# A one-core log-softmax over 50000 columns: the first tile's load cut into four column pieces, and one late store issued inside the next tile's exponentials

## The chip, the cores and the metric

The kernel runs on one core of one Trainium2 chip. The metric is the device time of one execution in microseconds (us). The seven runs of the kernel before took 7582.85, 7583.15, 7583.72, 7608.13, 7610.33, 7612.80 and 7635.38 us; their median is 7608.13 us. Besides them one execution was taken by the profiler, and every duration below comes from that one.

## The reference

The input is `x` with 16 x 512 x 50000 values in float32, so 8192 rows of 50000 columns, 1638.4 MB in and as much out.

```python
max_x = np.max(x, axis=-1, keepdims=True)
shifted = x - max_x
log_sum_exp = np.log(np.sum(np.exp(shifted), axis=-1, keepdims=True))
return (shifted - log_sum_exp).astype(np.float32)
```

## The kernel before

A tile is 32 rows. Each row is cut into four segments of 12500 columns, and each segment lies on a partition of its own, so a tile is 128 partitions x 12500 values, 6250 KB (50 KB a partition). There are 256 tiles, numbered 0 to 255 here, and four buffers (`NBUF`), each of a whole tile; a tile is loaded into its buffer, changed in place and stored from it. For the vector work a tile has four column pieces (`NS`) of 3125 columns, which `cols(c)` picks.

The order of the work is written by hand, engine by engine, with semaphores:

- SyncE (SP) issues the loads. Tiles 0 to 3 are loaded at once, each whole with one `dma_start` that raises `landed[j]` by 16. From then on, in a loop of 63 rounds over the four buffers, it waits for `stored[j]`, takes 16 off it and loads the next tile into buffer j. So load t+4 is issued when store t has landed.
- VectorE (DVE), in `whole(j)`, waits for `landed[j]` (through `take`, line 45), reduces each of the four pieces to a negated maximum (line 195), joins the four (line 200), shares the maximum among the four partitions of a row by transposes (`share`, lines 163 to 178), later multiplies the partial sums by their scales (line 206), and subtracts maximum and log-sum from the whole buffer with one instruction (line 183). In the last tile alone that subtraction is cut into four pieces.
- ScalarE (ACT), in its own `whole(j)`, takes the exponential of each piece with its own maximum and adds it up (line 234, one exponential behind each reduction), makes the scales (line 242) and the logarithm (line 225). After that it issues the store of the tile (line 229, `store`), which waits until DVE has subtracted. The store of the last tile goes out in four pieces.
- TensorE adds the four segments of a row by a matrix of ones (line 271).

Loads and stores are issued on two queues: the page's q1 carries the loads and q10 the stores. Each has its own transfers in order, and the 16 DMA engines work on both.

DVE and ACT run 63 rounds of four tiles in loops; the last four tiles (252 to 255) are written out behind the loops. Tile 252 is the fourth-last.

A count of events on a semaphore is kept by `Count`: `next` makes an instruction wait for the next event, so two instructions that wait on `subtracted` take its events in the order in which they are written.

Of the kernel before, what the change touches and what calls it, by code (L numbers as in the profile page):

```python
# [19 lines left out]
NBUF = 4  # L20

NS = 4


class Count:
# [17 lines left out]
def take(engine, sem, n=16):  # L43

    engine.wait_ge(sem, n).then_inc(sem, -n)  # L45


def cols(c):
    return slice(c * C, (c + 1) * C)
# [3 lines left out]
def kernel(  # L53
# [9 lines left out]
    W = V // G  # L63
    assert N % R == 0 and W == NS * C
    ntiles = N // R


    rounds = (ntiles - NBUF) // NBUF
    assert ntiles % NBUF == 0 and rounds >= 2

    xt = xf.rearrange("(t r) (g w) -> t (r g) w", r=R, g=G)
    ot = of.rearrange("(t r) (g w) -> t (r g) w", r=R, g=G)

    def run(a, first, n):

        part = a[first : first + NBUF * n].rearrange("(q i) p w -> q i p w", i=NBUF)
        return lambda q, i: part[bass.ds(q, 1), i].rearrange("o p w -> (o p) w")
# [13 lines left out]
    bufs = [data.tile([P, W], FP32, name=f"buf{j}") for j in range(NBUF)]  # L91
# [4 lines left out]
    def each(n, width, name):  # L96
        return [stats.tile([P, width], FP32, name=f"{name}{j}") for j in range(n)]

    negms, parts, scales, scaleds = (
        each(NBUF, NS, n) for n in ("negm", "part", "scale", "scaled")  # L100
    )
# [9 lines left out]
    def sem(name):  # L111
        return ctx.enter_context(nc.semaphore(name))

    landed = [sem(f"landed{j}") for j in range(NBUF)]
    stored = [sem(f"stored{j}") for j in range(NBUF)]
    ready = sem("ones_ready")
    on_dve = Count(sem("on_dve"))
    on_act = Count(sem("on_act"))
# [10 lines left out]
    @block.gpsimd  # L129
    def _(gpsimd):  # L130
        view = ones.rearrange("p (r g) -> p r g", g=G)
        gpsimd.memset(ones, 1.0).then_inc(ready)  # L132
        gpsimd.affine_select(  # L133
            out=view, in_=view, pattern=[[-G, R], [0, G]], base=0,
            channel_multiplier=1, compare_op=ALU.is_ge, fill=0.0,
        ).wait_op(ready, 1, "sem-ge").then_inc(ready)
        gpsimd.affine_select(  # L137
            out=view, in_=view, pattern=[[G, R], [0, G]], base=G - 1,
            channel_multiplier=-1, compare_op=ALU.is_ge, fill=0.0,
        ).wait_op(ready, 2, "sem-ge").then_inc(ready)  # L140

    @block.sync
    def _(sync):
        def load(j, src):
            sync.dma_start(out=bufs[j], in_=src).then_inc(landed[j], 16)

        for t in range(NBUF):
            load(t, xt[t])
        src = run(xt, NBUF, rounds)
        with sync.Fori(0, rounds) as q:  # L150
            for j in range(NBUF):
                take(sync, stored[j])
                load(j, src(q, j))
        for j in range(NBUF - 1):
            take(sync, stored[j])
        take(sync, stored[NBUF - 1], 16 * NS)

    @block.vector
    def _(vector):
        def share(k):  # L160

            on_dve.next(
                vector.transpose(out=allneg, in_=negp.to_broadcast([P, SQ]))  # L163
            ).then_inc(on_dve.sem)
            on_dve.next(
                vector.tensor_reduce(  # L166
                    out=rowneg, in_=allneg.rearrange("p (r g) -> p r g", g=G),
                    op=ALU.min, axis=AX,
                )
            ).then_inc(on_dve.sem)  # L170
            on_dve.next(
                vector.tensor_copy(  # L172
                    out=spread.rearrange("p (r g) -> p r g", g=G),
                    in_=rowneg[:, :, None].to_broadcast([P, SQ // G, G]),
                )
            ).then_inc(on_dve.sem)
            on_dve.next(
                vector.transpose(out=negmaxs[k], in_=spread)  # L178
            ).then_inc(agreed.sem)

        def subtract(k, *bufs):
            for n, buf in enumerate(bufs):
                ins = vector.tensor_scalar(  # L183
                    out=buf, in0=buf, scalar1=negmaxs[k][:, 0:1], scalar2=logs[k],
                    op0=ALU.add, op1=ALU.subtract,
                )
                if n == 0:
                    logged.next(ins)
                ins.then_inc(subtracted.sem)

        def whole(j, by_pieces=False):
            take(vector, landed[j])

            for c in range(NS):
                vector.tensor_reduce(  # L195
                    out=negms[j][:, c : c + 1], in_=bufs[j][:, cols(c)],
                    op=ALU.max, axis=AX, negate=True,
                ).then_inc(shifted.sem if c < NS - 1 else on_dve.sem)
            on_dve.next(vector.nop()).then_inc(shifted.sem)  # L199
            vector.tensor_reduce(  # L200
                out=negp, in_=negms[j], op=ALU.min, axis=AX
            ).then_inc(on_dve.sem)
            share(j)

            rescaled.next(
                vector.tensor_mul(out=scaleds[j], in0=scales[j], in1=parts[j])  # L206
            ).then_inc(summed.sem)
            subtract(j, *([bufs[j][:, cols(c)] for c in range(NS)] if by_pieces else [bufs[j]]))

        def settle():  # L210
            for count in (on_dve, rescaled, logged):
                count.settle(vector)

        with vector.Fori(0, rounds):
            for j in range(NBUF):
                whole(j)
            settle()
        for j in range(NBUF):
            whole(j, by_pieces=j == NBUF - 1)

    @block.scalar
    def _(scalar):
        def log(k):
            added.next(
                scalar.activation(out=logs[k], in_=rowsums[k], func=ACT.Ln)  # L225
            ).then_inc(logged.sem)

        def store(j, dst, buf):
            subtracted.next(scalar.dma_start(out=dst, in_=buf)).then_inc(stored[j], 16)

        def whole(j):
            for c in range(NS):
                shifted.next(
                    scalar.activation(  # L234
                        out=dump, in_=bufs[j][:, cols(c)], func=ACT.Exp,
                        bias=negms[j][:, c : c + 1], scale=1.0,
                        accum_out=parts[j][:, c : c + 1],
                    )
                ).then_inc(on_act.sem)
                on_act.next(scalar.nop())  # L240
            agreed.next(
                scalar.activation(  # L242
                    out=scales[j], in_=negms[j], func=ACT.Exp,
                    bias=negmaxs[j][:, 0:1], scale=-1.0,
                )
            ).then_inc(rescaled.sem)
            log(j)

        def settle():
            for count in (on_act, shifted, agreed, added, subtracted):  # L250
                count.settle(scalar)

        nc.scalar.preload_act_table_set("natural_log_exp_and_others")  # L253
        dst = run(ot, 0, rounds)
        with scalar.Fori(0, rounds) as q:
            for j in range(NBUF):
                whole(j)
                store(j, dst(q, j), bufs[j])
            settle()
        for j in range(NBUF - 1):  # L260
            whole(j)
            store(j, ot[ntiles - NBUF + j], bufs[j])
        whole(NBUF - 1)
        for c in range(NS):
            store(NBUF - 1, ot[ntiles - 1][:, cols(c)], bufs[NBUF - 1][:, cols(c)])
# [50 lines left out]
```

## Time and profile before

| what | value |
|---|---|
| median of the seven runs | 7608.13 us (7582.85 to 7635.38) |
| the profiled execution's own time | 7599.88 us |
| its span, first to last instruction | 7598.2 us |
| VectorE busy | 5441.1 us (72%) |
| ScalarE busy | 3184.7 us (42%) |
| TensorE matmul busy | 477.7 us (6%) |
| reductions, line 195 | 1024 of 3.40 us |
| exponentials, line 234 | 1024 of 2.87 us |
| whole-tile subtraction, line 183 | 6.79 us each |
| bytes moved | 1638.4 MB read, 1638.4 MB written |
| load, issue to landing, median | 44.1 us |
| whole-tile store, issue to landing, median | 48.0 us |

The page gives for each engine its busy time as a share of the span. Below that it cuts the span into 40 slices of 190 us and gives for each the mean busy share of the 16 DMA engines in tenths and the rate at which they moved bytes. The time from issue to landing of a transfer includes the time that it waits in its queue behind the transfer issued before it, and it ends when the last of the 16 engines has moved its part.

### The profile page before, as it was taken

To read this page: it belongs to the slowest core of one execution; us is meant where nothing else is said; L and a number is where in the kernel's file an instruction comes from. 1 tells how busy PE (TensorE), PEld (TensorE's weight loads), DVE (VectorE), ACT (ScalarE), POOL (GpSimd) and SP (SyncE) were. 2 spreads that over 40 slices of the span, in tenths; PEclk is the share of its full clock that TensorE was granted. 3 is DMA by queue.
4 is the path that set the end of the run, shared out by engine and by line. 5 is a ranking of instruction groups with operands and counts; after the bars stand their busy time and mean duration, and the time that the engine had idled before them with its cause. 6 is when DMAs were issued, how large, how long until landed. Compare 5 with 4: busy or idle time off the path is not lost. (4 is left out here: it accounts for less than half of the span.)

```text
span 7598.2 us, 14069 instructions
## 1 busy us (share of the span) xinstructions
PE 477.7 (6%) x2048; PEld 455.8 (6%) x2048; DVE 5441.1 (72%) x2819; ACT 3184.7 (42%) x2561; POOL 1.4 (0%) x7
## 2 busy tenths in 40 slices
PE   0000000000000000000000000000000000000000
PEld 0000000000000000000000000000000000000000
DVE  7777777777777777777777777777777777777776
ACT  4444344443434434344443444434344443444433
POOL 0000000000000000000000000000000000000000
DMA  9999999999999999999999999999999999999998
GB/s 415 433 434 434 434 434 434 434 434 434 432 434 432 433 433 434 434 434 434 432 434 434 434 434 434 434 434 433 433 433 434 434 431 433 433 429 431 430 429 383
DMA packets 74162, 3276.85 MB, mean 431 GB/s; under 512 B 8240, under 2 KB 8240, under 8 KB 8240
## 3 DMA queue, kind: packets, MB, share of 16 engines
q1 hardware_dynamic: 36864, 1638.42, 50.0%
q10 hardware_dynamic: 37296, 1638.42, 49.9%
q14 instruction: 2, 0.02, 0.0%
HBM read 1638.40 MB, written 1638.40 MB: 431 GB/s over the span
## 5 line engine op out<-in xcount | busy, mean ns | idle before, releaser
L234 ACT ACTIVATE dump<-buf,negm 128x3125 f32<-128x3125 f32 x1024 | 2937.2, 2868 | 3818.1 <-DVE negm L195 3720.7
L195 DVE TENSOR_REDUCE negm<-buf 128x1 f32<-128x3125 f32 x1024 | 3418.3, 3401 | 936.3 <-DVEq L45 936.3
L183 DVE TENSOR_SCALAR buf<-buf,negmax,logsum 128x12500 f32<-128x12500 f32 (+1 forms) x259 | 1738.9, 6715 | 553.5 <-ACT logsum L225 553.5
L271 PE MATMUL sums<-scaled,ones 128*128 128x1 f32 x2048 | 477.7, 355 | 7100.4 <-DVE scaled L206 7100.4
L271 PEld LDWEIGHTS sums<-scaled,ones 128*128 128x128 f32 x2048 | 455.8, 327 | 7122.2 <-DVE scaled L206 7122.2
L206 DVE TENSOR_TENSOR scaled<-scale,part 128x4 f32<-128x4 f32 x256 | 41.7, 163 | 580.1 <-ACT scale L242 580.1
L225 ACT ACTIVATE logsum<-sums 128x1 f32<-128x1 f32 x256 | 43.8, 171 | 550.9 <-PE sums L271 550.9
L234 ACT ACTIVATION_READ_ACCUMULATOR dump<-buf,negm 128x1 f32 x1024 | 190.8, 186 | 0.0
L242 ACT ACTIVATE scale<-negm,negmax 128x4 f32<-128x4 f32 x256 | 76.1, 297 | 23.6
L200 DVE TENSOR_REDUCE negp<-negm 128x1 f32<-128x4 f32 x256 | 40.2, 157 | 39.2 <-DVE negm L195 39.2
L163 DVE STREAM_TRANSPOSE allneg<-negp 128x32 f32<-128x32 f32 x256 | 54.1, 212 | 8.9
L178 DVE STREAM_TRANSPOSE negmax<-spread 128x32 f32<-128x32 f32 x256 | 54.1, 211 | 8.9
L166 DVE TENSOR_REDUCE rowneg<-allneg 128x8 f32<-128x32 f32 x256 | 47.7, 186 | 8.9
L172 DVE COPY spread<-rowneg 128x32 f32<-128x32 f32 x256 | 46.5, 182 | 8.9
L253 ACT ACT_TABLE_LOAD x1 | 1.3, 1283 | 1.0 <-SPq L109 1.0
L133 POOL TENSOR_SCALAR_AFFINE_SELECT ones<-ones 128x128 f32<-128x128 f32 x1 | 0.5, 517 | 0.1
L137 POOL TENSOR_SCALAR_AFFINE_SELECT ones<-ones 128x128 f32<-128x128 f32 x1 | 0.5, 517 | 0.1
L132 POOL MEMSET ones<- 128x128 f32 x1 | 0.2, 204 | 0.5 <-SPq L109 0.5
L300 POOL MEMSET const-bfloat16-1.0<- 128x1 bf16 x1 | 0.1, 102 | 0.0
L300 POOL MEMSET const-uint8-127<- 128x1 uint8 x1 | 0.1, 102 | 0.0
L300 POOL MEMSET const-float32-0.0<- 128x1 f32 x1 | 0.1, 99 | 0.3 <-issue 0.3
L300 POOL MEMSET const-float32-1.0<- 128x1 f32 x1 | 0.1, 99 | 0.0
## 6 DMA issues: line engine op xcount, KB each, us to landing
buf<-in_x_dram SPq DMA_DIRECT2D x256, 6250.0 KB, 44.1
out_dram<-buf ACTq DMA_DIRECT2D x255, 6250.0 KB, 48.0
out_dram<-buf ACTq DMA_DIRECT2D x4, 1562.5 KB, 8.1
```

The lines of the kernel that those rows point to most:

```text
L163: vector.transpose(out=allneg, in_=negp.to_broadcast([P, SQ]))
L166: vector.tensor_reduce(out=rowneg, in_=allneg.rearrange("p (r g) -> p r g", g=G), op=ALU.min, axis=AX,)
L172: vector.tensor_copy(out=spread.rearrange("p (r g) -> p r g", g=G), in_=rowneg[:, :, None].to_broadcast([P, SQ // G, G]),)
L178: vector.transpose(out=negmaxs[k], in_=spread)
L183: ins = vector.tensor_scalar(out=buf, in0=buf, scalar1=negmaxs[k][:, 0:1], scalar2=logs[k], op0=ALU.add, op1=ALU.subtract,)
L195: vector.tensor_reduce(out=negms[j][:, c : c + 1], in_=bufs[j][:, cols(c)], op=ALU.max, axis=AX, negate=True,).then_inc(shifted.sem if c < ...
L200: vector.tensor_reduce(out=negp, in_=negms[j], op=ALU.min, axis=AX).then_inc(on_dve.sem)
L206: vector.tensor_mul(out=scaleds[j], in0=scales[j], in1=parts[j])
L225: scalar.activation(out=logs[k], in_=rowsums[k], func=ACT.Ln)
L234: scalar.activation(out=dump, in_=bufs[j][:, cols(c)], func=ACT.Exp, bias=negms[j][:, c : c + 1], scale=1.0, accum_out=parts[j][:, c : c + 1],
L242: scalar.activation(out=scales[j], in_=negms[j], func=ACT.Exp, bias=negmaxs[j][:, 0:1], scale=-1.0,)
L271: ins = tensor.matmul(rowsums[j], ones, scaleds[j][:, c : c + 1], start=c == 0, stop=c == NS - 1,)
```

## The change

Three things change.

- The load of tile 0 is issued as four transfers of 3125 columns each, in the order of the columns, and each raises a semaphore of its own (`pieces[c]`). DVE's `whole` has a new argument `in_pieces`: for tile 0 it waits for one piece ahead of each reduction, in place of the whole tile ahead of the first. Loads 1 to 3 follow behind the four pieces.
- To give tile 0 its own code, DVE's first round of four tiles is written out ahead of its loop, which then runs 62 rounds.
- On ScalarE the store of tile 252 is no longer issued behind that tile's logarithm. It is held, and issued in tile 253 between the third exponential and the fourth (`HELD = 3`). The stores of tiles 253, 254 and 255 stand where they did.

```diff
@@ sync
-        for t in range(NBUF):
+        for c in range(NS):
+            sync.dma_start(
+                out=bufs[0][:, cols(c)], in_=xt[0][:, cols(c)]
+            ).then_inc(pieces[c], 16)
+        for t in range(1, NBUF):
             load(t, xt[t])
@@ vector
-        def whole(j, by_pieces=False):
-            take(vector, landed[j])
+        def whole(j, in_pieces=False, by_pieces=False):
+            if not in_pieces:
+                take(vector, landed[j])
 
             for c in range(NS):
+                if in_pieces:
+                    take(vector, pieces[c])
                 vector.tensor_reduce(
...
-        with vector.Fori(0, rounds):
+        for j in range(NBUF):
+            whole(j, in_pieces=j == 0)
+        settle()
+        with vector.Fori(0, rounds - 1):
             for j in range(NBUF):
                 whole(j)
             settle()
@@ scalar
-        def whole(j):
+        def whole(j, held=None):
             for c in range(NS):
+                if c == HELD and held is not None:
+                    store(*held)
                 shifted.next(
...
-        for j in range(NBUF - 1):
+        whole(0)
+        whole(1, held=(0, ot[ntiles - NBUF], bufs[0]))
+        store(1, ot[ntiles - NBUF + 1], bufs[1])
+        for j in range(2, NBUF - 1):
             whole(j)
             store(j, ot[ntiles - NBUF + j], bufs[j])
         whole(NBUF - 1)
```

More of the change, by code (lines that the diff above doesn't have):

```diff
@@ L22 @@
 NS = 4
+HELD = 3
 class Count:
@@ L68 @@
     rounds = (ntiles - NBUF) // NBUF
-    assert ntiles % NBUF == 0 and rounds >= 2
+    assert ntiles % NBUF == 0 and rounds >= 3
     xt = xf.rearrange("(t r) (g w) -> t (r g) w", r=R, g=G)
@@ L115 @@
     stored = [sem(f"stored{j}") for j in range(NBUF)]
+    pieces = [sem(f"piece{c}") for c in range(NS)]
     ready = sem("ones_ready")
```

## The prediction

> **What bounds the kernel now.** I read the head of the page first. The core's own engines have room (VectorE, DVE, the fullest, is busy 72%), while the DMA engines are full in all 40 slices but the last.
>
> ```profile
> span 7598.2 us, 14069 instructions
> DMA  9999999999999999999999999999999999999998
> GB/s 415 433 434 434 434 434 434 434 434 434 432 434 432 433 433 434 434 434 434 432 434 434 434 434 434 434 434 433 433 433 434 434 431 433 433 429 431 430 429 383
> ```
>
> The reader is to see a kernel bound by bytes: 434 GB/s nearly throughout. Only three places are poorer: the first slice (415), the last (383), and a slow sag to 429 to 431 just before it. Next I read the loads' issues in two stretches, which give the period of a tile, then one store of each.
>
> ```profile
> L145 SPq DMA_DIRECT2D buf<-in_x_dram x20: 332/333/333, 1026.5 to 1587.1; - x20
> DMA to landing us min/median/max: 39.7/40.2/40.6
> ...
> L145 SPq DMA_DIRECT2D buf<-in_x_dram x14: 332/333/333, 7126.1 to 7514.1; - x14
> DMA to landing us min/median/max: 44.2/44.6/45.3
> ```
>
> Early, a tile takes (1587.1 - 1026.5)/19 = 29.51 us; late, (7514.1 - 7126.1)/13 = 29.85. The first is 12.8 MB in and out at 434 GB/s. The third view is the table of stretches (start:end, length, busy us of each engine, granted clock, DMA share, GB/s).
>
> ```profile
> 44.00:60.00 16.00, 0.00 (x0) 0.00 (x0) 15.38 (x10) 10.45 (x7) 0.00 (x0) 1.00 1.02 391
> 60.00:64.00 4.00, 1.85 (x8) 1.78 (x8) 0.16 (x1) 1.81 (x3) 0.00 (x0) 1.00 0.75 238
> 64.00:100.00 36.00, 1.88 (x9) 1.78 (x8) 31.02 (x13) 12.61 (x11) 0.00 (x0) 1.00 1.00 396
> ...
> 7546.00:7555.40 9.40, 1.87 (x8) 1.78 (x8) 6.89 (x2) 0.47 (x2) 0.00 (x0) 1.00 0.12 53
> 7555.60:7571.00 15.40, 0.00 (x0) 0.00 (x0) 11.83 (x4) 7.74 (x5) 0.00 (x0) 1.00 0.96 416
> 7571.50:7580.30 8.80, 1.87 (x8) 1.78 (x8) 4.08 (x9) 4.19 (x6) 0.00 (x0) 1.00 0.05 23
> 7582.00:7596.00 14.00, 0.00 (x0) 0.00 (x0) 3.71 (x3) 0.00 (x0) 0.00 (x0) 1.00 1.02 429
> ```
>
> Two things are to be seen. When the first store joins the loads, 56 us pass at a lower rate: 16 x 391 + 4 x 238 + 36 x 396 = 21.5 MB, 49.5 us' worth, so 6.5 us are lost. And in the tail there are two holes, with a share of 0.12 and of 0.05. One engine of 16 is a share of 0.06: in the holes one or two engines are still working while the others have run out. Some engine lags the rest, and it has no hole.
>
> The sum for the span: first bytes at 2.0 us (the stretch 0 to 2 has none), 256 x 29.51 = 7554.6, 6.5 for the start of the stores, 1.5 behind the last bytes: 7564.6. The other 33.6 us are the sag and its lag. The execution's own time is 7599.88, 1.7 over its span; it lies 8.2 below the median of the seven runs (7608.13), between three runs at 7583 and three at 7608 to 7613.
>
> **The change: the first tile in pieces.** Its place in the timeline (start, length, engine, line):
>
> ```profile
> 19.19 13.35 DVE L195 TENSOR_REDUCE negm<-buf 128x1 f32<-128x3125 f32 x4 [19.19 <-DVEq L45]
> 45.20 0.40 ACTq L229 DMA_DIRECT2D out_dram<-buf  x1
> ...
> 151.03 13.35 DVE L195 TENSOR_REDUCE negm<-buf 128x1 f32<-128x3125 f32 x4 [2.34 <-DVEq L45]
> 177.03 0.34 ACTq L229 DMA_DIRECT2D out_dram<-buf  x1
> ```
>
> Load 0 is issued at 1.03 and used at 19.19. A quarter of its bytes takes 29.51/8 = 3.7 us alone, so the pieces land at about 8.0, 11.7, 15.4 and 19.1; the reductions (3.40 each) keep pace, and the last ends at 22.5, not 32.54. Store 0 is issued at 35.2, 10.0 us earlier. The added SP work, three more issues of 0.42 us, is over by 3.7 us, long before load 1's bytes are wanted (its turn comes at about 17). Cover: load 0's own transfer. If the bytes of the pieces came slower, each us would come off the 10.0 and off nothing else. DVE's three more waits have the reductions queued behind them, and ACT's exponentials behind those; both are ahead of the old time in any case. The written-out round changes no work of DVE, and DVE waits 936.3 us in all for loads (3.7 a tile), which covers a few more instructions.
>
> What are the 10.0 us worth? Of bytes, nothing: the DMA engines have loads 1 to 3 to carry till then, and first bytes come at 2.0 as before. DVE reaches its first wait for a load sooner than at 148.72. The 6.5 us of the start is a price I can't see at the new place: it could vanish (-6.5) or double (+6.5). I take 0, since reads meet their first writes in both kernels.
>
> The Trainium skill ("DMA: Bandwidth & Descriptors", the section on the anatomy of one DMA) gives each transfer a fixed 2.0 us, which speaks against cutting a load. Against it stands the stretch 7582 to 7596 above, four piece transfers at 429 GB/s with no gap. By the rule, as an estimate, three more transfers one behind the other would add 6 us.
>
> **The shift.** A tile goes round in load (39.0 us for ten loads from 318), compute (26.0, from 151.03 to 177.03) and store (52.6 for ten stores from 324): 117.6, four periods. A transfer at half the rate needs 29.5, so load and store wait 9.5 and 23.1 behind the one in front. The total is fixed by the buffers; the change moves it. A store queue that starts 10.0 us sooner takes bytes from the loads, and its lead over them turns into waiting of the loads: I estimate 10 to 20 us (10.0 if only the issue moves, 20 if it costs the loads the same bytes again). Stores then wait 3 to 13 us, loads 20 to 30.
>
> That matters at the end only:
>
> ```profile
> 7494.97 0.35 ACTq L229 DMA_DIRECT2D out_dram<-buf  x1
> 7512.01 0.19 ACT L234 ACTIVATION_READ_ACCUMULATOR dump<-buf,negm 128x1 f32 x1
> 7512.58 2.87 ACT L234 ACTIVATE dump<-buf,negm 128x3125 f32<-128x3125 f32 x1 [0.38 <-DVEq L199]
> 7555.49 0.34 ACTq L229 DMA_DIRECT2D out_dram<-buf  x1
> 7559.17 13.35 DVE L195 TENSOR_REDUCE negm<-buf 128x1 f32<-128x3125 f32 x4 [3.71 <-DVEq L45]
> 7580.30 5.79 ACTq L229 DMA_DIRECT2D out_dram<-buf  x4
> ```
>
> The last load has landed at 7559.1; the last tile's first piece is issued at 7580.3, 21.2 us later. Store 254, issued at 7555.49, lands 25.8 us later, at 7581.3. So the lagging engine has work for 22.2 us and never stops. With stores 10 to 20 us nearer their issue, 5 to 10 us of that work is already done when the last load lands: pieces alone uncover 4 to 9 us.
>
> **The held store.** Store 252 moves from 7494.97 to about 7512.2, 17.2 us. It does not wait there (its subtraction is over) and costs ACT one issue of 0.34 us within the 0.38 that ACT idles anyway; uncovered, 0.34 on tile 253, whose store queues in any case. It gates no load. A store queue that waits 3 to 13 us would stand empty for 4 to 14; meanwhile loads run at twice the rate, the last lands 2 to 7 us earlier and 2 to 7 us more of stores are left behind it: 4 to 14 us of cover against the 4 to 9 missing. So the hold gives back the loss and no more: the lagging engine had no hole to fill. Its price runs from 0 to 17.2, the latter if the loads ran dry too; I take 0, as loads 254 and 255 then lie in their queue.
>
> Sum: 0 (head) + 0 (start) + 5 to 10 uncovered, taken back by the hold = 0. **Forecast: 7600 us**, no change.
>
> **Rivals.**
>
> *Slower: the sag comes early.* Place: the middle of the run; price 0.34 us a tile, the late period against the early. With loads now queued deep and stores short, the queue that runs dry on the engines that are ahead is the stores', and these engines read alone. If that is what made the period 29.85, it starts at once: 256 x 0.34 = 87, of which 33.6 are in the sum: +53, 7653. It decides the sign as soon as some 92 more tiles (31 us) run at 29.85. For: the period did grow while load waits grew, from 39.0 to 44.6. Against: 4 to 44 us, loads alone, ran at 436 GB/s.
>
> *Faster: the sag goes.* With the other split of waits the engines stay level: 7600 less most of 33.6. Three of the seven runs at 7583 show what the same program takes when little is lost; with the start's 6.5 gone too, 7576. For: the sag is no fixed cost, slices 3 to 10 have none. Against: nothing in the change touches a rate.
>
> *The hold does nothing.* The store before it, issued at 7465.2, lands 48.7 us later at 7513.9, behind 7512.2: with waits as before, the held store would stand in line anyway. If the shift is small, nothing is uncovered either (7600); if large and the hold fails, 4 to 9 us: 7604 to 7609. Both count as no change.
>
> **How the numbers follow.** A difference under 0.3% (23 us) can't be told from none here. No change, the idle hold included: 0.55. Faster 0.30: the sag gone, helped by the three runs at 7583, which alone lie 0.33% under the median. Slower by over 0.3%: 0.15, the early sag. The time is that of the first case, 7600. Low: 7576, from the faster rival. High: 7600 + 9 uncovered + 17.2 for a hold that starves the queues = 7626. The early sag, 0.15, is left out.
>
> **What would show it.** Store 0 issued near 35; the first DVE wait for a load well before 148; loads that take 49 to 59 us to land and stores 33 to 43, with an unchanged 117.6 for the round; store 252 issued behind the third exponential of tile 253; no stretch of the tail with a DMA share of 0. The forecast falls if slices 3 to 30 leave 433 to 434, or if the tail behind the last load's landing is not 38 to 40 us.

## The result, and the profile after

| | median, us | lowest to highest | runs |
|---|---|---|---|
| before | 7587.23 | 7572.93 to 7635.38 | 58 |
| changed | 7605.90 | 7586.82 to 7620.20 | 24 |

The changed kernel is slower: the ratio is 1.0019, with a 95% interval of 1.0012 to 1.0027, so 0.19% or some 14 us (the medians differ by 18.7, the means by 14.6). 27 of the 58 runs of the kernel before took less than 7586 us, and none of the 24 of the changed kernel did. With 58 runs of the kernel before its median has come down from the 7608.13 of the first seven to 7587.23; 22 of its runs lie close together at 7582 to 7585.5, with a tail upward, and 12 are as slow as the profiled one or slower. That profiled execution (7599.88 us) was itself 12.7 above the median. The changed kernel's profiled execution took 7602.87.

The page of the changed kernel: the span, the rate in 40 slices, and the two DMA queues (packets, MB, the time of their packets as a share of 16 engines' span; q1 loads, q10 stores).

```profile
span 7601.2 us, 14073 instructions
...
GB/s 425 433 433 433 433 433 433 434 432 432 433 431 433 431 433 434 434 434 429 430 428 431 431 430 432 430 433 431 434 434 433 434 434 431 429 431 430 429 429 407
...
q1 hardware_dynamic: 37296, 1638.42, 50.3%
q10 hardware_dynamic: 37296, 1638.42, 49.8%
```

The same two lines of the kernel before, whose span was 7598.2:

```profile
q1 hardware_dynamic: 36864, 1638.42, 50.0%
q10 hardware_dynamic: 37296, 1638.42, 49.9%
```

The reader is to see where the time went. The bytes are the same, but the loads' packets took 50.3% of 7601.2 = 3823 us of each engine in place of 3799, while the stores' took 3785 in place of 3791 (a tenth of a per cent is 7.6 us, so each is good to 4). And the sag, which the kernel before showed mainly near its end, is there from the ninth slice on, in patches: 428 to 432 in slices 19 to 26, 433 to 434 again in slices 29 to 33, 429 to 431 later.

The head of the timeline (start, length, engine, line):

```profile
8.10 3.41 DVE L205 TENSOR_REDUCE negm<-buf 128x1 f32<-128x3125 f32 x1 [8.10 <-DVEq L47]
11.84 3.41 DVE L205 TENSOR_REDUCE negm<-buf 128x1 f32<-128x3125 f32 x1 [0.33 <-DVEq L47]
15.55 3.41 DVE L205 TENSOR_REDUCE negm<-buf 128x1 f32<-128x3125 f32 x1 [0.30 <-DVEq L47]
19.32 3.41 DVE L205 TENSOR_REDUCE negm<-buf 128x1 f32<-128x3125 f32 x1 [0.36 <-DVEq L47]
...
35.38 0.40 ACTq L242 DMA_DIRECT2D out_dram<-buf  x1
...
90.51 13.35 DVE L205 TENSOR_REDUCE negm<-buf 128x1 f32<-128x3125 f32 x4 [3.39 <-DVEq L47]
```

The four pieces come into use 3.7 us apart, which is the time of their bytes and nothing more. The Trainium skill ("DMA: Bandwidth & Descriptors", the section on the anatomy of one DMA) gives a fixed 2.0 us for each transfer that GpSimd issues; these loads are issued by SyncE, and no such time shows between them. Store 0 is issued at 35.38 in place of 45.20; and DVE waits for a load at 90.5 already, not first at 151. So the head does what it was meant to do.

Four loads issued from 130 to 220, and four stores issued from 260 to 360, with their times from issue to landing:

```profile
L148 SPq DMA_DIRECT2D buf<-in_x_dram x4: 332/332/333, 130.6 to 219.2; - x4
DMA to landing us min/median/max: 48.6/49.7/50.4
L242 ACTq DMA_DIRECT2D out_dram<-buf x4: 338/338/344, 266.0 to 355.3; - x4
DMA to landing us min/median/max: 41.0/41.2/41.5
```

Some 11 us have moved from the stores (52.6 before) to the loads (39.0 before); with 26.0 of compute the round is 116.9.

That is the split of the waiting near the start. Near the end, where the prediction needs it, far less is left of it. The last three loads of pieces_only (the change without the held store) and of the kernel before, with their times from issue to landing:

```profile
L148 SPq DMA_DIRECT2D buf<-in_x_dram x3: 332/332/333, 7452.7 to 7511.9; - x3
DMA to landing us min/median/max: 47.9/47.9/47.9
...
L145 SPq DMA_DIRECT2D buf<-in_x_dram x3: 332/332/333, 7454.2 to 7514.1; - x3
DMA to landing us min/median/max: 44.8/45.0/45.3
```

The kernel before had come from 39.0 to 45.0 by itself, and pieces_only is only 2.9 us above it; the two whole stores issued in the same stretch land after 44.1 us in place of 48.9.

The tail:

```profile
7517.19 0.19 ACT L249 ACTIVATION_READ_ACCUMULATOR dump<-buf,negm 128x1 f32 x1
7517.46 0.35 ACTq L242 DMA_DIRECT2D out_dram<-buf  x1
7517.86 2.87 ACT L249 ACTIVATE dump<-buf,negm 128x3125 f32<-128x3125 f32 x1 [0.48 <-DVEq L209]
...
7559.12 13.35 DVE L205 TENSOR_REDUCE negm<-buf 128x1 f32<-128x3125 f32 x4 [2.85 <-DVEq L47]
7580.24 5.79 ACTq L242 DMA_DIRECT2D out_dram<-buf  x4
```

Store 252 is issued behind the third exponential of tile 253 and costs ScalarE 0.1 us. From the last load's landing (7559.1) to the end of the span are 42.1 us; before it was 39.1. The stretches (start:end, length, busy us of each engine, granted clock, DMA share, GB/s), the last of them beside that of the kernel before:

```profile
20.00:44.00 24.00, 1.86 (x8) 1.78 (x8) 19.28 (x11) 10.42 (x9) 0.00 (x0) 1.00 0.99 404
44.00:60.00 16.00, 1.86 (x8) 1.78 (x8) 11.28 (x9) 7.46 (x8) 0.00 (x0) 1.00 1.03 444
60.00:100.00 40.00, 1.87 (x8) 1.78 (x8) 31.89 (x15) 18.16 (x13) 0.00 (x0) 1.00 0.99 426
...
1600.00:2800.00 1200.00, 74.65 (x320) 71.23 (x320) 863.51 (x444) 506.40 (x407) 0.00 (x0) 1.00 1.00 432
2800.00:3200.00 400.00, 26.14 (x112) 24.94 (x112) 284.20 (x150) 165.09 (x134) 0.00 (x0) 1.00 1.00 434
3200.00:4800.00 1600.00, 100.81 (x432) 96.18 (x432) 1147.70 (x594) 671.50 (x540) 0.00 (x0) 1.00 1.00 431
6400.00:7450.00 1050.00, 65.33 (x280) 62.34 (x280) 748.71 (x388) 436.50 (x351) 0.00 (x0) 1.00 1.00 430
7450.00:7601.00 151.00, 9.33 (x40) 8.90 (x40) 102.03 (x57) 60.92 (x50) 0.00 (x0) 1.00 0.94 402
```

```profile
7450.00:7601.00 151.00, 9.34 (x40) 8.91 (x40) 96.01 (x55) 55.43 (x46) 0.00 (x0) 1.00 0.85 365
```

The start of the stores is cheaper than before: from 20 to 100, 24 x 404 + 16 x 444 + 40 x 426 = 33.8 MB or 78.0 us' worth at 434, so 2.0 us are lost, where the kernel before lost 6.5. The loss lies in the long middle, where the DMA engines are always busy and yet move 430 to 432 GB/s over long stretches. The two profiled executions differ by only 3.0 us of span, because that of the kernel before lost its time elsewhere: at the start of the stores, and in the holes of its tail. Its DMA engines were busy 0.85 of these last 151 us in place of 0.94, some 13 us less (3 of them behind its end).

### The profile page after: what moved, and what is told of

It reads as the page before. It is cut to its first block, busy times and chain, and to the rows that moved or that the text cites. A ratio compares the mean times of both kernels' runs of the same rounds, so it can differ in the third digit from the quotient of the medians.

```text
span 7601.2 us, 14073 instructions
## 1 busy us (share of the span) xinstructions
PE 477.9 (6%) x2048; PEld 456.0 (6%) x2048; DVE 5441.5 (72%) x2819; ACT 3184.7 (42%) x2561; POOL 1.4 (0%) x7
## 3 DMA queue, kind: packets, MB, share of 16 engines
q1 hardware_dynamic: 37296, 1638.42, 50.3%
q10 hardware_dynamic: 37296, 1638.42, 49.8%
## 5 line engine op out<-in xcount | busy, mean ns | idle before, releaser
L173 DVE TENSOR_REDUCE rowneg<-allneg 128x8 f32<-128x32 f32 x256 | 47.7, 186 | 8.9
## 6 DMA issues: line engine op xcount, KB each, us to landing
out_dram<-buf ACTq DMA_DIRECT2D x255, 6250.0 KB, 44.1
buf<-in_x_dram SPq DMA_DIRECT2D x4, 1562.5 KB, 11.8
```

The costliest lines, as they stand in the source:

```text
L173: vector.tensor_reduce(out=rowneg, in_=allneg.rearrange("p (r g) -> p r g", g=G), op=ALU.min, axis=AX,)
```

## The experiments

Three causes were open: the hold (tail), the code and transfers that the pieces add, and the early first store. The kernels were measured in four groups, each beside its own runs of the kernel before, whose median was 7591.2, 7589.3, 7586.2 and 7589.8 us (below the first two rows, which repeat the result above, the rows are in the order of the groups: four, four, two and three). "Reads" is the share of q1 on the page times the span, good to 4 us. "Loads land after" is the median time from issue to landing of the loads issued between 130 and 240 us. Both are of the one profiled execution.

| kernel | stores 0, 1, 2 issued at, us | median, us | ratio, 95% interval | loads land after, us | reads, us |
|---|---|---|---|---|---|
| before | 45, 71, 97 | 7587.2 | | 39.1 | 3799 |
| changed | 35, 61, 87 | 7605.9 | 1.0019, 1.0012 to 1.0027 | 49.7 | 3823 |
| pieces_only | 35, 61, 87 | 7601.8 | 1.0015, 1.0001 to 1.0028 | 48.8 | 3815 |
| hold_only | as before | 7587.1 | 1.0001, 0.9982 to 1.0019 | 39.6 | 3793 |
| late_first_store | 45, 61, 87 | 7593.0 | 0.9999, 0.9984 to 1.0014 | 41.3 | 3807 |
| written_out_only | as before | 7584.0 | 0.9992, 0.9979 to 1.0006 | 38.8 | 3795 |
| pieces_waited | 45, 71, 96 | 7584.6 | 0.9988, 0.9970 to 1.0006 | 40.4 | 3789 |
| mid_first_store | 42, 61, 87 | 7595.1 | 0.9997, 0.9978 to 1.0017 | 36.8 | 3802 |
| later_first_store | 58, 71, 97 | 7580.4 | 0.9982, 0.9964 to 1.0001 | 37.9 | 3791 |
| earlier_first_store | 30, 61, 87 | 7601.6 | 0.9998, 0.9971 to 1.0025 | 37.0 | 3813 |
| pieces_later | 54, 61, 87 | 7594.2 | 1.0005, 0.9993 to 1.0018 | 36.9 | 3802 |
| later_again | 59, 72, 97 | 7581.9 | 0.9990, 0.9978 to 1.0003 | 38.5 | 3790 |
| old_store_times | 45, 71, 97 | 7582.0 | 0.9992, 0.9981 to 1.0002 | 38.5 | 3790 |
| later_two | 58, 84, 97 | 7609.1 | 1.0031, 1.0019 to 1.0044 | 37.1 | 3814 |
| after_again | 35, 61, 87 | 7610.7 | 1.0025, 1.0014 to 1.0035 | 48.8 | 3824 |

**Pieces without the hold (pieces_only).**

```diff
-        whole(0)
-        whole(1, held=(0, ot[ntiles - NBUF], bufs[0]))
-        store(1, ot[ntiles - NBUF + 1], bufs[1])
-        for j in range(2, NBUF - 1):
+        for j in range(NBUF - 1):
             whole(j)
             store(j, ot[ntiles - NBUF + j], bufs[j])
```

> The pieces without the held store. Split theory (the earlier first store moves waiting from the stores to the loads, and that other split makes reads slow all through the run): as slow as the changed kernel or up to 9 us slower, 1.002 to 1.003; loads near tile 10 land 49 us after issue, stores 42; the rate of the middle slices sags before slice 9. Hold theory (the loss is in the tail, from store 252 being late): 1.000. In both, the span behind the last load's landing grows from 39 to 42 to 48 us, since the tail is uncovered.

1.0015, and the interval just leaves out 1: the loss is there without the hold. Its page has the patches of sag too, and more reading time than before:

```profile
GB/s 425 433 433 433 433 433 432 433 434 434 433 434 434 433 434 434 434 433 434 430 432 430 434 434 433 433 434 434 434 430 431 433 430 429 429 430 429 426 428 400
...
q1 hardware_dynamic: 37296, 1638.42, 50.2%
```

Its tail was not longer: the last reductions begin at 7559.94 and the span ends at 7599.0, 39.1 us as before. The 4 to 9 us that I had thought uncovered did not appear. They were worked out from a shift of 10 to 20 us, and of the shift 3 to 5 us were left by then.

**The hold alone (hold_only).** The change's edits on ScalarE's last tiles, made to the kernel before.

```diff
...
-        for j in range(NBUF - 1):
+        whole(0)
+        whole(1, held=(0, ot[ntiles - NBUF], bufs[0]))
+        store(1, ot[ntiles - NBUF + 1], bufs[1])
+        for j in range(2, NBUF - 1):
```

> Store 252 held, first tile loaded whole. Split theory: 1.000, for store 252 waits some 20 us in its queue anyway and the hold is 17.2. Hold theory: 1.002, and a hole in the DMA share between 7490 and 7520.

1.0001, 7587.1 us. The hold does open a hole, the DMA share is 0.35 from 7490 to 7500, but the time is that of before as far as can be told. In the profiled executions the tail from the last load's landing to the end is 40.6 us here and 42.1 in the changed kernel, against 39.1 without the hold (before, pieces_only; later_again, also without it, has 40.6). If the hold costs these 1.5 to 3 us, they are too few to be seen in the medians. The interval reaches 1.0019, so the time alone does not rule the hold out as the cause; the reads at 3793 us and pieces_only do.

**Store 0 at its old time (late_first_store)**, everything else as changed: with FIRST = 2 it is issued behind tile 1's second exponential.

```diff
-        def whole(j, held=None):
+        def whole(j, held=None, at=HELD):
...
-                if c == HELD and held is not None:
+                if c == at and held is not None:
...
+        whole(0)
+        whole(1, held=(0, ot[0], bufs[0]), at=FIRST)
+        store(1, ot[1], bufs[1])
+        for j in range(2, NBUF):
+            whole(j)
+            store(j, ot[j], bufs[j])
+        settle()
-        dst = run(ot, 0, rounds)
-        with scalar.Fori(0, rounds) as q:
+        dst = run(ot, NBUF, rounds - 1)
+        with scalar.Fori(0, rounds - 1) as q:
```

> The changed kernel with one thing more: store 0 is issued within tile 1 behind its second exponential, at about 45.3 us as in the kernel before, though tile 0 is still loaded in pieces and computed 10 us early. Split theory: the old split is back (load near tile 10 lands 39 us after issue, store 52.6), the early slices are at 434, and the time is that of the kernel before, 1.000. Theory that the pieces or the written-out code cost it: 1.002. Hold theory: 1.002.

0.9999, 7593.0 us: some of the loss is gone, with 4 of 12 runs under 7585. The old split is nearly back (loads 41.3, stores 49.8), but the profiled run still reads slowly in several slices. So the median said yes and the reads said not quite; the split theory was left with a doubt.

**The written-out round alone (written_out_only).**

```diff
-        with vector.Fori(0, rounds):
+        for j in range(NBUF):
+            whole(j)
+        settle()
+        with vector.Fori(0, rounds - 1):
```

> VectorE's first round of four tiles written out ahead of its loop, nothing else. Split theory and hold theory: 1.000. Code theory (longer program, instruction loading): 1.002.

0.9992, 7584.0 us (interval up to 1.0006). No cost of the longer program can be seen.

**Pieces, but used late (pieces_waited).**

```diff
-                if in_pieces:
-                    take(vector, pieces[c])
+                if in_pieces and c == 0:
+                    for piece in pieces:
+                        take(vector, piece)
```

> The changed kernel, but the first reduction waits for all four pieces, so the first tile is computed and stored as late as before; load in pieces, written-out round and held store stay. Split theory (an earlier first store moves waiting from stores to loads, and with that split reads are slow through the run): 1.000, load near tile 10 lands 39 us after issue. Pieces theory (four transfers in place of one cost it): 1.002. Start-pattern theory (the time hangs on the pattern in which the start leaves the 16 DMA engines, not on the split): anything from 0.999 to 1.003, unrelated to the split.

0.9988, 7584.6 us, reads 3789. The interval ends at 1.0006, so no cost of four transfers in place of one can be seen, and none of the hold that is still in: this is the whole change without its early first tile.

**Store 0 between old and new (mid_first_store).** The edit of late_first_store with FIRST = 1.

> The changed kernel with store 0 issued within tile 1 behind its first exponential, at about 42 us, between the changed kernel's 35.4 and the old 45.2. Split theory: loads near tile 10 land 42 to 46 us after issue and the ratio lies between, 1.000 to 1.0015. Start-pattern theory: unrelated to the split.

The median lies between, 7595.1, with no run of 11 under 7585; the ratio, 0.9997 with an interval of 0.9978 to 1.0017, can't tell. But the split did not follow: loads land after 36.8 us and stores after 55.0, on the far side of the old split, and the reads are slow all the same, from the sixth slice on. The first lines are four loads issued from 130 to 240:

```profile
GB/s 425 434 434 433 433 432 431 432 432 432 432 431 432 429 431 429 429 430 432 434 433 434 434 434 434 434 434 434 433 434 434 434 434 434 434 434 433 434 434 405
...
L149 SPq DMA_DIRECT2D buf<-in_x_dram x4: 332/332/333, 135.6 to 224.7; - x4
DMA to landing us min/median/max: 36.7/36.8/37.3
```

By this the split theory falls as it was put: it is not that loads wait long that makes reads slow. From slice 20 on the same kernel moves 433 to 434: the lower rate is one that a run can leave.

**Store 0 later than before (later_first_store).** The kernel before, with store 0 behind the third exponential of tile 1 (the first round written out on ScalarE as above).

```diff
...
+        whole(0)
+        whole(1, held=(0, ot[0], bufs[0]))
+        store(1, ot[1], bufs[1])
...
```

> The kernel before with store 0 issued within tile 1 behind its third exponential, at about 58 us in place of 45.2; nothing else. Split theory: loads wait still less (landing 30 to 39 us after issue), stores more; reads are no slower than before and the ratio is 0.998 to 1.000. Start-pattern theory: unrelated to the split; 1.001 or more would speak for it.

0.9982, and 0.9990 when it was run again; both intervals just reach 1, so that it is faster is not shown. 11 of its 15 runs lie under 7585.

> The kernel before with store 0 behind tile 1's third exponential (about 58 us), once more, to narrow the interval. Start theory: 0.998 to 0.9995. If its first result was chance: 1.000.

**Store 0 earlier still (earlier_first_store).** Tile 0 is also subtracted and stored in four pieces, and the next load into its buffer waits for all four stores.

```diff
-            whole(j, in_pieces=j == 0)
+            whole(j, in_pieces=j == 0, by_pieces=j == 0)
...
+        for c in range(NS):
+            store(0, ot[0][:, cols(c)], bufs[0][:, cols(c)])
```

> The changed kernel with tile 0 also subtracted and stored in four pieces, so its first store is issued at about 30.5 us, 5 us sooner still. Split theory: loads near tile 10 land 52 to 58 us after issue, reads are as slow as in the changed kernel or slower, 1.002 to 1.004. Start-pattern theory: unrelated to the split; 1.000 would speak for it.

7601.6 us, reads 3813, though the ratio's interval is wide (0.9971 to 1.0025; the runs of before in that group reached 7683), so the time alone shows no loss. Here too the split went the other way than I expected (loads 37.0, stores 55.5), with 428 to 432 GB/s in slices 8 to 17, the second blow to the split.

**Pieces with store 0 at 54 (pieces_later).** Store 0 is issued behind tile 1's logarithm, directly ahead of store 1.

> The changed kernel with store 0 issued only behind tile 1's logarithm, at about 54.4 us, when loads 0 to 2 have landed; first tile still in pieces and computed early. Start theory (what counts is when the first store joins the loads; up to 42 us leaves reads slow through the run, from 45 us on mostly not): 0.998 to 1.000, most runs at 7579 to 7590, the reads' share of the DMA time at 50.0 to 50.1%. Theory that the early compute or the pieces cost it: 1.0015 to 1.002.

7594.2, with no run of four under 7590, but the interval (0.9993 to 1.0018) takes in 1. The reads, 3802 us, are more than with stores 1 and 2 at their old times, here 3790 (later_again): a hint, from one execution each, that the time of store 0 alone does not decide it.

**Each store in two halves (after_halves, before_halves).** My guess was that the slow reads go with the moments at which the engines pass from one store to the next, so I doubled these moments.

```diff
+        def halves(j, dst, buf):
+            store(j, dst[: P // 2], buf[: P // 2])
+            scalar.dma_start(out=dst[P // 2 :], in_=buf[P // 2 :]).then_inc(stored[j], 16)
...
```

> The changed kernel with every store of tiles 0 to 251 issued as two transfers of 64 partitions each (same bytes, same packets, one after the other), so there are twice as many change-overs from one store to the next. Change-over theory (reads are slowed while the engines pass from one store to the next): 1.003 to 1.005 against before, the reads' share 50.5% or more. Theory that the slow reads only coincide with change-overs: 1.002 as the changed kernel.

> The kernel before with the same halves. Change-over theory: little or nothing while the start leaves the reads undisturbed, 1.000 to 1.001, and so less than the halves cost the changed kernel. If an extra transfer has a price of its own, both kernels lose the same.

Both were 17% slower: 1.1696 (1.1659 to 1.1734) and 1.1681 (1.1643 to 1.1720). That answers another question than the one asked. Two stretches of after_halves and its queues:

```profile
400.00:1600.00 1200.00, 65.30 (x280) 62.30 (x280) 738.55 (x385) 435.24 (x350) 0.00 (x0) 1.00 0.99 370
6000.00:7000.00 1000.00, 52.26 (x224) 49.86 (x224) 612.47 (x318) 359.78 (x287) 0.00 (x0) 1.00 0.99 369
...
q10 hardware_dynamic: 41328, 1638.43, 51.3%
q1 hardware_dynamic: 37296, 1638.42, 47.7%
```

The engines are as full as ever and move 370 GB/s. The packets of both queues take longer: 51.3% of 8808.0 us is 4518 for the stores and 47.7% is 4201 for the loads, against 3785 and 3823 in the changed kernel. Whether it is the half of the partitions or the doubled number of transfers that does it was not separated, so the price of a change-over can't be read from it.

**All three first stores at their old times (old_store_times)**, measured together with later_two and with the changed kernel once more (after_again). The first tile is still loaded in pieces and computed early.

```diff
...
+        whole(0)
+        whole(1, held=(0, ot[0], bufs[0]), at=FIRST)
+        whole(2, held=(1, ot[1], bufs[1]), at=FIRST)
+        whole(3, held=(2, ot[2], bufs[2]), at=FIRST)
+        store(3, ot[3], bufs[3])
...
```

> The changed kernel with stores 0, 1 and 2 each issued within the next tile behind its second exponential: at about 45, 71 and 97 us, the times of the kernel before, while the first tile is still loaded in pieces and computed 10 us early. Store-time theory (the loss comes from when the first stores join the loads): 1.000, at 7582 to 7590, the reads' share 50.0%. Early-compute theory (something else in computing the first tiles early costs it): 1.0008 to 1.002, 7593 or more.

> The changed kernel once more on the same chip as the two others, as their yardstick: 1.0012 to 1.0027 if the record holds; the reads' share near 50.3%, and more of it in the middle slices than in the first.

7582.0 against the changed kernel's 7610.7, measured together, so 28.7 us from three stores issued 10 us later (0.9992 against 1.0025; the intervals do not touch). The edit also writes ScalarE's first round ahead of its loop; later_two, below, has that too and is slow, so it is not the cure. The page and three stretches of old_store_times, and two lines of after_again:

```profile
GB/s 414 433 434 433 434 434 433 434 434 434 433 434 434 434 433 434 434 434 432 434 434 434 433 434 434 434 432 434 435 434 433 433 434 434 433 434 434 434 433 397
...
q1 hardware_dynamic: 37296, 1638.42, 50.0%
...
1600.00:2800.00 1200.00, 76.56 (x328) 73.05 (x328) 862.26 (x451) 509.83 (x410) 0.00 (x0) 1.00 1.00 434
3200.00:4800.00 1600.00, 100.79 (x432) 96.16 (x432) 1151.73 (x596) 675.29 (x543) 0.00 (x0) 1.00 1.00 434
6400.00:7450.00 1050.00, 67.22 (x288) 64.13 (x288) 751.40 (x391) 438.30 (x354) 0.00 (x0) 1.00 1.00 434
```

```profile
GB/s 424 431 433 434 433 433 433 433 433 433 433 432 432 433 433 433 432 432 433 432 432 431 429 431 428 432 428 432 430 431 429 431 430 429 431 434 434 434 434 408
...
q1 hardware_dynamic: 37296, 1638.42, 50.3%
```

Where the changed kernel moved 430 to 432, this one moves 434 in each stretch. Its start is as dear as before (381 and 384 GB/s from 44 to 100), so the cheaper start of the changed kernel went with the dearer run.

**Stores 0 and 1 later than before (later_two).** Tile 2 carries store 1 behind its third exponential.

```diff
...
+        whole(0)
+        whole(1, held=(0, ot[0], bufs[0]))
+        whole(2, held=(1, ot[1], bufs[1]))
+        store(2, ot[2], bufs[2])
...
```

> The kernel before with store 0 at about 58 us and store 1 at about 84 us (within tile 2, behind its third exponential) in place of 45 and 71. Store-time theory: as good as with store 0 alone at 58 or better, 0.997 to 0.9995. If the later start costs the DMA engines idle time: 1.000 to 1.002.

1.0031 (1.0019 to 1.0044), against both expectations, and with a sag again:

```profile
GB/s 415 433 432 432 434 433 433 433 433 433 433 433 431 431 430 430 432 430 430 432 431 432 430 435 430 431 433 431 433 433 433 433 433 433 433 433 433 433 433 379
...
q1 hardware_dynamic: 36864, 1638.42, 50.1%
```

Idle time at the start is not the reason: from 44 to 100 it moves 416 and 374 GB/s, 21.6 MB, where the kernel before moved 21.5. So later is not better by rule. What counts is the pattern of the first three stores against the loads, and no simple direction in time.

One column of the table sorts all the rows, though no theory had forecast it: where the loads issued between 130 and 240 us land after 37.9 to 40.4 us, the reads take 3789 to 3795 us (3799 in the kernel before, with its late sag); where they land after 37.1 or less, or after 41.3 or more, the reads take 3802 to 3824. With 4 us of error on each the two sides just meet. This is a band found afterwards in fifteen executions, and no cause is shown by it. It is not a rule for the whole run either: the median load of old_store_times lands after 44.1 us, and it moves 434 GB/s in each of the stretches above.

## Why the prediction was wrong, point by point

- **What bounds the kernel** was right: DMA bytes throughout. A change at the head or tail can only move time if it changes the engines' rate, or the time that they stand idle at the two ends.
- **The head in pieces** was right to a fifth of a us: pieces in use at 8.1, 11.8, 15.6 and 19.3 (8.0, 11.7, 15.4, 19.1 forecast), store 0 at 35.4 (35.2).
- **The shift of waiting** was right in size near the start: loads 49.7 (49 to 59 forecast), stores 41.2 (33 to 43). That it would last was wrong: at the last loads and stores of pieces_only 3 to 5 us were left of it, and the prediction needed it there. That long waits of the loads make the slow reads, as I thought after the result, is refuted: mid_first_store and earlier_first_store have loads at 37 us and the slow reads.
- **The held store**: nothing that the medians show, but not because it gave back a loss of the tail. pieces_only has the same 39.1 us behind the last load as the kernel before, so the 4 to 9 us (5 to 10 in the line of the sum) were not there to give back, and with the hold the tail is 42.1.
- **The signs of being wrong** both came: slices left 433 to 434, and the tail left 38 to 40 us. The first was badly chosen, for the kernel before has slices at 432 as well (11, 13 and 20).
- **The start of the stores**: I took 0 between -6.5 and +6.5; it was 4.5 better (2.0 lost in place of 6.5).
- **The step that failed** is the one that reads "Of bytes, nothing", with the rate taken as untouched: "Nothing in the change touches a rate", I wrote against the faster rival, and believed it for the forecast too. The early first stores do touch it. The reads' packets took 3823 us of each engine (3824 when run again) where they took 3790 in old_store_times, some 33 us more. The spans of these executions differ by 21 and 22 us and the medians by 28.7, so the slower reads are of the size of the loss; they need not equal it, since the packets of loads and stores overlap in part (50.3% and 49.8% are more than the whole).
- **The slower rival**, a sag that comes early, was what happened. Its price was too high (53 us; the medians differ by 18.7). Its reason, engines that read alone behind a deep load queue, does not cover mid_first_store, earlier_first_store and later_two, whose loads wait less than before and whose reads are slow too. I gave it 0.15 against 0.55 for no change; the loss is under the 0.3% that I took for the least that can be told, and with 58 and 24 runs it can be told.
- **The base**: 7600 was the profiled execution, which sagged toward its end. Most runs of the same program take less, and its median is 7587.2. An execution with a term of 33.6 us that I could not assign was a poor zero; that 7600 came within 6 us of the new time was luck, because that execution was an unlucky one.

What stays open is why the pattern matters. In the packet records of the traces the median 50 KB packet of a load takes 1.85 us in every kernel here. What differs is how many take more than 1.9 us, of some 32700: 102 in pieces_waited, 184 in old_store_times, 903 in the kernel before, 1679 and 1960 in the two executions of the changed kernel. What delays these few is not shown, and the one experiment on a possible reason, the change-overs between stores, could not answer it. Whether store 0 alone, early with stores 1 and 2 at their old times, would be enough was not tried.

## What to carry to other kernels

When DMA engines are full all the time, work started earlier gives nothing by itself, and what is left to win or lose is the rate at which both directions run together, and the idle time at the two ends; look at the share of time of the loads and of the stores, and at the slices, not at the waits. Before a profiled execution is taken as the base of a sum, compare it with many runs: where many runs lie close together and the others form a tail above them, an unexplained remainder in the sum may belong to the tail. And test "when" apart from "what": holding a few stores back to their old times, with all else changed, showed here what the experiments before it had left open.

## What the runs showed of the hardware that was not expected

- The times at which the first three stores meet the loads bear on the rate for thousands of us: 434 GB/s (old_store_times) or 430 to 432 in long stretches (changed), with the same bytes and the same engine share. A run can leave either rate: mid_first_store moves 429 to 432 in slices 6 to 19 and 433 to 434 from slice 20 on, and the kernel before falls from 434 to 429 near its end.
- With the stores of tiles 0 to 251 cut into two transfers of 64 partitions each, both directions together move 370 GB/s in place of 434, though the packets are as long in bytes as before.
- Four loads in place of one, 1.6 MB each, come into use 3.7 us apart, and no cost of them can be seen (pieces_waited, 0.9970 to 1.0006).
